# Binary cross entropy on one core: the 32-row side block is loaded at launch instead of near the end

## The chip, the core and the metric

The kernel runs on one core of a Trainium2 chip. A core has a vector engine (VectorE, DVE in the profile), a scalar engine (ScalarE, ACT), GpSimd (POOL) and a sync engine (SP); 16 DMA engines move data between HBM and the on-chip memory, SBUF, which has 128 partitions. A transfer is issued by an instruction on one engine's queue. Here those are POOL's queue (called software_dynamic in the profile, queue q0) and SP's (hardware_dynamic, q1). The metric is the time of one execution on the device in microseconds (us); lower is better.

## The reference

```
pred = np.clip(pred, eps, 1 - eps)          # eps = 1e-7
return -(target * np.log(pred) + (1 - target) * np.log(1 - pred))
```

`pred` and `target` are 8192 x 8192 float32, and so is the result. The targets are 0 or 1, so exactly one of the two logarithms counts for an element. The kernel uses this: with p the clipped prediction and t the target, |t - 1 + p| is p where t is 1, and 1 - p where t is 0. The result is minus the logarithm of that.

## The kernel before

The 67.1 million elements are cut into 37 blocks that lie one behind the other in the flat arrays. Each block is spread over 128 partitions. Blocks 0 and 1 are 7680 columns wide, blocks 2 to 33 have 15360 columns, blocks 34 and 35 again 7680, block 36 has 1696. A block of 15360 columns is 7.86 MB of float32. A remainder of 32 x 1408 elements at the very end of the arrays is the side block: it lies in two small tiles of 32 partitions, `side_p` and `side_t`.

`ring_p` (float32) and `ring_t` (bfloat16) hold two halves of 15360 columns and a small piece for block 36. Even blocks use one half and odd blocks the other. A block is worked on in place and stored from `ring_p`, so the next block that uses the same half is loaded once the store has landed.

- `load(k)` (lines 78 to 81) issues the targets on POOL's queue, which turns them into bfloat16 on the way, and the predictions, also on POOL's queue, except for block 0, whose predictions go through SP's.
- `front` (lines 98 to 106) clips on DVE (L99), adds t - 1 on DVE (L102), and takes the absolute value (L105) and the logarithm (L106) on ACT.
- `back` (L109) changes the sign on DVE.
- `store(k)` (lines 83 to 85) goes through POOL's queue, and through SP's for the last three blocks.
- `load_side` (lines 87 to 92) first writes two columns of `side_p` and `side_t` on DVE, and then issues eight loads on SP. Each moves eight rows of 1408 float32, 44 KB: rows j, j+4, ..., j+28 of the 32, for j from 0 to 3, the targets and the predictions in turn. `store_side` (lines 94 to 96) issues four such stores on SP.

The order on each engine is the order of the program text (a manual schedule). At launch the blocks 0, 1 and 2 are loaded. Blocks 0 and 1 are computed and stored, and block 3 is loaded into their half. Then the loop over blocks 2 to 32 does the front and the back of a block in two pieces, stores it, and loads block k + 2 into the same half. On POOL the store of block k, the targets of block k + 2 and the predictions of block k + 2 thus follow each other; the last one waits until the store has landed. Block 31 is the place (n - 6, with n = 37) where `load_side` is called, behind the store of that block in the text; the side block's front comes behind block 32's back, its sign change and its stores behind the first half of block 33's front. The two columns that DVE writes there keep the eight loads on SP from being issued before DVE has come to that place.

Of the kernel before, what the change touches and what calls it, by code (L numbers as in the profile page):

```python
# [1 line left out]

# [4 lines left out]

EPS = 1e-7

BIG = 15 * 1024
HALF = BIG // 2
SIDE = 1408


def plan(total):

    n, last = divmod(total, BIG)
    assert n > 4 and 0 < last <= 2048
    spots = [(HALF, 0), (HALF, HALF)]
    spots += [(BIG, k % 2 * BIG) for k in range(1, n - 1)]
    end = (n - 1) % 2 * BIG
    return spots + [(HALF, end), (HALF, end + HALF), (last - SIDE // 4, 2 * BIG)]

@with_exitstack  # L30
def kernel(
    ctx: ExitStack,
    tc: tile.TileContext,
    pred: bass.AP,
    target: bass.AP,
    out: bass.AP,
):

    nc = tc.nc
    fp32 = mybir.dt.float32
    bf16 = mybir.dt.bfloat16
    Alu = mybir.AluOpType
    Act = mybir.ActivationFunctionType
    P = nc.NUM_PARTITIONS

    R, C = pred.shape
    spots = plan(R * C // P)
    n = len(spots)
    widths = [w for w, _ in spots]
    cols = [sum(widths[:k]) for k in range(n)]

    def chunk(ap, k):
        flat = ap.rearrange("r c -> (r c)")
        return flat[cols[k] * P : (cols[k] + widths[k]) * P].rearrange("(p w) -> p w", p=P)

    pool = ctx.enter_context(tc.tile_pool(name="rings", bufs=1))
    ring = [P, 2 * BIG + widths[-1]]
    ring_p = pool.tile(ring, fp32, name="ring_p", tag="ring_p")
    ring_t = pool.tile(ring, bf16, name="ring_t", tag="ring_t")
    warm = pool.tile([1, 8], fp32, name="warm", tag="warm")
    side_p = pool.tile([32, SIDE], fp32, name="side_p", tag="side_p")
    side_t = pool.tile([32, SIDE], fp32, name="side_t", tag="side_t")

    def side(ap, j):
        flat = ap.rearrange("r c -> (r c)")  # L70
        return flat[R * C - 32 * SIDE :].rearrange("(p w) -> p w", p=32)[j:32:4]

    def spot(ring, k, part=(0, 1)):
        w, c = spots[k]
        i, m = part
        return ring[:, c + i * w // m : c + (i + 1) * w // m]

    def load(k):
        queue = nc.sync if k == 0 else nc.gpsimd
        nc.gpsimd.dma_start(out=spot(ring_t, k), in_=chunk(target, k))  # L80
        queue.dma_start(out=spot(ring_p, k), in_=chunk(pred, k))  # L81

    def store(k):
        queue = nc.sync if k >= n - 3 else nc.gpsimd
        queue.dma_start(out=chunk(out, k), in_=spot(ring_p, k))  # L85

    def load_side():
        nc.vector.memset(side_p[:, 0:2], 0.5)  # L88
        nc.vector.memset(side_t[:, 0:2], 0.0)  # L89
        for j in range(4):  # L90
            nc.sync.dma_start(out=side_t[j:32:4, :], in_=side(target, j))
            nc.sync.dma_start(out=side_p[j:32:4, :], in_=side(pred, j))

    def store_side():
        for j in range(4):
            nc.sync.dma_start(out=side(out, j), in_=side_p[j:32:4, :])

    def front_of(p, t):
        nc.vector.tensor_scalar(  # L99
            out=p, in0=p, scalar1=EPS, scalar2=1 - EPS, op0=Alu.max, op1=Alu.min  # L100
        )
        nc.vector.scalar_tensor_tensor(  # L102
            out=p, in0=t, scalar=1.0, in1=p, op0=Alu.subtract, op1=Alu.add
        )
        nc.scalar.activation(out=p, in_=p, func=Act.Abs)  # L105
        nc.scalar.activation(out=p, in_=p, func=Act.Ln)  # L106

    def back_of(p):
        nc.vector.tensor_scalar(out=p, in0=p, scalar1=-1.0, scalar2=None, op0=Alu.mult)  # L109

    def front(k, *part):
        front_of(spot(ring_p, k, *part), spot(ring_t, k, *part))

    def back(k, *part):
        back_of(spot(ring_p, k, *part))

    with tc.manual_schedule():
        nc.vector.memset(warm, 1.0)  # L118
        for k in range(3):
            load(k)  # L120
        nc.scalar.activation(out=warm, in_=warm, func=Act.Ln)  # L121
        front(0)
        front(1)
        back(0)
        store(0)
        back(1)
        store(1)
        load(3)
        for k in range(2, n - 4):
            front(k, (0, 2))  # L130
            front(k, (1, 2))
            back(k, (0, 2))
            back(k, (1, 2))
            store(k)
            if k == n - 6:
                load_side()
            if k == n - 5:
                front_of(side_p, side_t)
            for j in range(k + 2, n if k == n - 5 else k + 3):
                load(j)  # L140
        z, a, b, c = range(n - 4, n)
        front(z, (0, 2))
        back_of(side_p)
        store_side()
        front(z, (1, 2))
        back(z, (0, 2))
        front(a)
        back(z, (1, 2))
        store(z)
        front(b, (0, 2))  # L150
        front(b, (1, 2))
        back(a)
        store(a)
        front(c)
        back(b)
        store(b)
        back(c)
        store(c)


# [1 line left out]
_INS = ['pred', 'target']  # L162
_OUTS = [((8192, 8192), 'float32')]


# [23 lines left out]
```

## Time and profile before

| | us |
|---|---|
| median of 3 runs | 1864.86 |
| lowest and highest | 1864.77, 1866.35 |
| span of the profiled execution, first to last instruction | 1864.5 |
| DVE busy | 1124.7 |
| ACT busy | 902.1 |
| POOL busy | 57.6 |

The profile is of one execution, whose span is 0.4 us below the median of the runs; no other time of that execution is given. Its times count from the start of the span. A line of the timeline or of the chain of waits gives the start, the duration, the engine, the line of the kernel (L102 is line 102) and the operation with what it writes and reads; in brackets stands how long the engine had been idle and what ended that. The row "DMA" on the page cuts the span into 40 slices and gives the busy share of the 16 DMA engines in tenths (9 is 90% or more). A table of stretches gives, for each, the busy time of the engines, then the granted clock of the matrix engine (not used here), the DMA share and the GB/s moved, counted on the SBUF side, where a converted target has half its bytes. These shares are approximate, here and there a little above 1.

Of the transfers, the page shows that POOL's queue moves 657.98 MB (98.5% of the time of the 16 engines) and SP's 13.21 MB (1.7%). A load of a large prediction block takes 35.9 us from issue to landing in the median, a store 29.2 us, a load of targets 46.8 us.

### The profile page before, as it was taken

The page shows a single profiled execution, that of the slowest core. Times are in us where ns is not written, and L with a number is a line of the kernel's source. Part 1 is how long each engine was busy: PE and PEld are TensorE (multiplying, and loading weights), DVE is VectorE, ACT ScalarE, POOL GpSimd, SP SyncE. Part 2 cuts the span into 40 slices and gives each one's busy share as a digit, 9 for nine tenths or more (in the row PEclk, how much of TensorE's full clock was granted, in tenths as well). Part 3 has the DMA queues.
Part 4 walks back from the last instruction along what each step waited for, and adds up shares of the span by engine and source line. Part 5 has one row for each costly group of instructions (what it writes and reads, how often), then busy time and mean ns, then how long its engine had stood idle before and what let it go on. Part 6 is the DMA issues. An engine that isn't in the chain of part 4 may idle for free.

```text
span 1864.5 us, 649 instructions
## 1 busy us (share of the span) xinstructions
DVE 1124.7 (60%) x215; ACT 902.1 (48%) x144; POOL 57.6 (3%) x111
## 2 busy tenths in 40 slices
DVE  4655766555576655567665556766555576655585
ACT  3345553335555334555433355553335555333665
POOL 0000000000000000000000000000000000000000
DMA  9999999999999999999999999999999999999999
GB/s 295 369 355 349 348 348 368 382 385 347 351 348 348 370 380 382 343 357 344 352 370 384 386 340 356 352 345 370 382 385 345 349 355 344 371 382 386 346 341 391
DMA packets 16180, 671.22 MB, mean 360 GB/s; under 512 B 1872, under 2 KB 1872, under 8 KB 2352
## 3 DMA queue, kind: packets, MB, share of 16 engines
q0 software_dynamic: 15408, 657.98, 98.5%
q1 hardware_dynamic: 768, 13.21, 1.7%
q14 instruction: 4, 0.03, 0.0%
HBM read 536.87 MB, written 268.44 MB: 432 GB/s over the span
## 4 chain that ended last, share of the span: by engine, by line
DMA 35%; issue 26%; ACT 22%; DVE 15%; POOL 1%; DVEq 0%; POOLq 0%; PEldq 0%
DMA ring_p<-in_pred_dram 32%; ACT ring_p L105 11%; ACT ring_p L106 11%; DVE ring_p L102 7%; DVE ring_p L99 4%; DVE ring_p L109 4%; DMA out_dram<-ring_p 3%; POOL ring_t L80 0%; POOL out_dram L85 0%; DVEq L184 0%; POOL ring_p L81 0%; POOLq L85 0%; POOLq L80 0%; DVEq L99 0%; PEldq L184 0%
## 5 line engine op out<-in xcount | busy, mean ns | idle before, releaser
L105 ACT ACTIVATE ring_p<-ring_p 128x7680 f32<-128x7680 f32 (+1 forms) x70 | 450.3, 6433 | 933.6 <-DVE ring_p L102 933.6
L102 DVE SCALAR_TENSOR_TENSOR ring_p<-ring_t,ring_p 128x7680 f32<-128x7680 bf16 (+1 forms) x70 | 556.8, 7955 | 2.4
L99 DVE TENSOR_SCALAR ring_p<-ring_p 128x7680 f32<-128x7680 f32 (+1 forms) x70 | 283.8, 4054 | 398.2 <-DMA ring_p<-in_pred_dram 398.2
L109 DVE TENSOR_SCALAR ring_p<-ring_p 128x7680 f32<-128x7680 f32 (+1 forms) x69 | 283.8, 4114 | 321.2 <-ACT ring_p L106 321.2
L106 ACT ACTIVATE ring_p<-ring_p 128x7680 f32<-128x7680 f32 (+1 forms) x70 | 450.8, 6440 | 2.2
L81 POOL DMA_DIRECT2D ring_p<-in_pred_dram x36 | 19.3, 535 | 910.0 <-DMA out_dram<-ring_p 910.0
L85 POOL DMA_DIRECT2D out_dram<-ring_p x34 | 18.3, 539 | 851.7 <-DVE ring_p L109 827.4
L80 POOL DMA_DIRECT2D ring_t<-in_target_dram x37 | 20.4, 550 | 0.8 <-PEq L184 0.8
L105 ACT ACTIVATE side_p<-side_p 32x1408 f32<-32x1408 f32 x1 | 1.4, 1375 | 6.7 <-DVE side_p L102 6.7
L121 ACT ACT_TABLE_LOAD x1 | 1.3, 1283 | 0.7 <-PEq L173 0.7
L102 DVE SCALAR_TENSOR_TENSOR side_p<-side_t,side_p 32x1408 f32<-32x1408 f32 x1 | 1.6, 1611 | 0.0
L106 ACT ACTIVATE side_p<-side_p 32x1408 f32<-32x1408 f32 x1 | 1.4, 1375 | 0.0
L109 DVE TENSOR_SCALAR side_p<-side_p 32x1408 f32<-32x1408 f32 x1 | 0.9, 875 | 0.0
L99 DVE TENSOR_SCALAR side_p<-side_p 32x1408 f32<-32x1408 f32 x1 | 0.9, 874 | 0.0
L118 DVE MEMSET warm<- 1x8 f32 x1 | 0.1, 65 | 0.8 <-PEq L173 0.8
L121 ACT ACTIVATE warm<-warm 1x8 f32<-1x8 f32 x1 | 0.2, 208 | 0.0
L173 POOL MEMSET const-float32-0.0<- 128x1 f32 x1 | 0.1, 98 | 0.2 <-issue 0.2
L173 POOL MEMSET const-bfloat16-1.0<- 128x1 bf16 x1 | 0.1, 101 | 0.0
L173 POOL MEMSET const-float32-1.0<- 128x1 f32 x1 | 0.1, 98 | 0.0
L173 POOL MEMSET const-uint8-127<- 128x1 uint8 x1 | 0.1, 98 | 0.0
L88 DVE MEMSET side_p<- 32x2 f32 x1 | 0.1, 60 | 0.0
L89 DVE MEMSET side_t<- 32x2 f32 x1 | 0.1, 60 | 0.0
## 6 DMA issues: line engine op xcount, KB each, us to landing
ring_p<-in_pred_dram POOLq DMA_DIRECT2D x32, 7680.0 KB, 35.9
out_dram<-ring_p POOLq DMA_DIRECT2D x32, 7680.0 KB, 29.2
ring_t<-in_target_dram POOLq DMA_DIRECT2D x32, 3840.0 KB, 46.8
ring_p<-in_pred_dram POOLq DMA_DIRECT2D x3, 3840.0 KB, 35.7
ring_t<-in_target_dram POOLq DMA_DIRECT2D x4, 1920.0 KB, 28.1
out_dram<-ring_p POOLq DMA_DIRECT2D x2, 3840.0 KB, 27.6
out_dram<-ring_p SPq DMA_DIRECT2D x2, 3840.0 KB
ring_p<-in_pred_dram SPq DMA_DIRECT2D x1, 3840.0 KB
```

Of the source, the lines that this page charges most:

```text
L80: nc.gpsimd.dma_start(out=spot(ring_t, k), in_=chunk(target, k))
L81: queue.dma_start(out=spot(ring_p, k), in_=chunk(pred, k))
L85: queue.dma_start(out=chunk(out, k), in_=spot(ring_p, k))
L88: nc.vector.memset(side_p[:, 0:2], 0.5)
L89: nc.vector.memset(side_t[:, 0:2], 0.0)
L99: nc.vector.tensor_scalar(out=p, in0=p, scalar1=EPS, scalar2=1 - EPS, op0=Alu.max, op1=Alu.min)
L102: nc.vector.scalar_tensor_tensor(out=p, in0=t, scalar=1.0, in1=p, op0=Alu.subtract, op1=Alu.add)
L105: nc.scalar.activation(out=p, in_=p, func=Act.Abs)
L106: nc.scalar.activation(out=p, in_=p, func=Act.Ln)
L109: nc.vector.tensor_scalar(out=p, in0=p, scalar1=-1.0, scalar2=None, op0=Alu.mult)
L121: nc.scalar.activation(out=warm, in_=warm, func=Act.Ln)
L173: nc = _bacc.Bacc("TRN2", target_bir_lowering=False, num_devices=1)
```

## The change

`load_side` is called at launch, directly behind the load of block 0 and ahead of the loads of blocks 1 and 2, and no longer in the loop at block 31. The two writes of DVE in it are gone. All else stays: the same eight loads on SP's queue, the same place of the side block's computation and of its stores. Blank lines are removed, so line numbers in the changed kernel are lower: L99, L102, L105, L106 and L109 become L86, L89, L92, L93 and L96; the loads of a block become L69 and L70, its store L74, the loads of the side block L78 and L79, its stores L83.

```
     def load_side():
-        nc.vector.memset(side_p[:, 0:2], 0.5)
-        nc.vector.memset(side_t[:, 0:2], 0.0)
         for j in range(4):
             nc.sync.dma_start(out=side_t[j:32:4, :], in_=side(target, j))
             nc.sync.dma_start(out=side_p[j:32:4, :], in_=side(pred, j))
...
         nc.vector.memset(warm, 1.0)
-        for k in range(3):
-            load(k)
+        load(0)
+        load_side()
+        load(1)
+        load(2)
         nc.scalar.activation(out=warm, in_=warm, func=Act.Ln)
...
             store(k)
-            if k == n - 6:
-                load_side()
             if k == n - 5:
                 front_of(side_p, side_t)
```

## The prediction

> **What bounds the kernel now.** I read the page's busy shares first, then the slices of the span, then the chain that ended last, then the transfers by window.
>
> ```profile
> DVE 1124.7 (60%) x215; ACT 902.1 (48%) x144; POOL 57.6 (3%) x111
> ...
> DMA  9999999999999999999999999999999999999999
> ...
> HBM read 536.87 MB, written 268.44 MB: 432 GB/s over the span
> ```
>
> No compute engine is busy for more than 60% of the span, while the 16 DMA engines are at nine tenths or more in all 40 slices. The chain of waits looks at first like a loop of latencies instead. Here is one turn of it, in order of time (start, duration, what):
>
> ```profile
> 1675.80 35.94 DMA ring_p<-in_pred_dram
> 1711.76 4.17 DVE ring_p L99
> ...
> 1750.54 4.17 DVE ring_p L109
> ...
> 1755.00 29.20 DMA out_dram<-ring_p
> ...
> 1784.48 18.53 DMA ring_p<-in_pred_dram
> ```
>
> A prediction block lands, DVE and ACT work on it for 43 us, it is stored, and the store's landing frees its half of the ring for the next load. Two such loops are interleaved, one for each half. Whether the loop or the bandwidth sets the pace is told by the stretches of one block each (length, DVE, ACT, POOL busy, clock, DMA share, GB/s):
>
> ```profile
> 57.00:78.00 21.00, 4.61 (x2) 8.74 (x2) 1.48 (x3) 1.00 1.01 413
> ...
> 97.00:151.00 54.00, 31.98 (x7) 25.45 (x4) 1.16 (x3) 1.00 0.98 357
> ...
> 1567.00:1621.00 54.00, 32.53 (x7) 25.97 (x5) 1.61 (x3) 1.00 1.01 364
> ...
> 1676.00:1730.00 54.00, 32.51 (x9) 25.94 (x5) 1.39 (x3) 1.00 1.00 364
> ```
>
> The DMA share is 0.98 to 1.01 at the start, in the middle and in the stretch that now holds the side loads. So the 28 and 36 us in the loop are time in a queue that never runs dry. One block reads 7.86 MB of predictions and 7.86 MB of targets (float32 in HBM, halved on the way in) and writes 7.86 MB; 23.59 MB in the steady period of 54.35 us is 434 GB/s. All 805.3 MB at that rate take 1855.5 us. The rest of the 1864.5 us span is accounted for: about 1.5 us before the first packet (three empty slices of 0.5 us when the transfers are cut to the first 20), 3.7 us of missing DMA share in the last 18.5 us (80.1% there), and a wobble of 3.4 us early on. That wobble is in the issues of the prediction loads on POOL:
>
> ```profile
> 96.31 0.54 POOL L81 DMA_DIRECT2D ring_p<-in_pred_dram  x1 [24.98 <-DMA out_dram<-ring_p]
> ...
> 150.92 0.54 POOL L81 DMA_DIRECT2D ring_p<-in_pred_dram  x1 [29.05 <-DMA out_dram<-ring_p]
> ...
> 206.19 0.53 POOL L81 DMA_DIRECT2D ring_p<-in_pred_dram  x1 [29.44 <-DMA out_dram<-ring_p]
> ...
> 697.59 0.53 POOL L81 DMA_DIRECT2D ring_p<-in_pred_dram  x1 [29.08 <-DMA out_dram<-ring_p]
> ...
> 1675.80 0.53 POOL L81 DMA_DIRECT2D ring_p<-in_pred_dram  x1 [28.41 <-DMA out_dram<-ring_p]
> ...
> 1730.16 0.53 POOL L81 DMA_DIRECT2D ring_p<-in_pred_dram  x1 [28.46 <-DMA out_dram<-ring_p]
> ```
>
> The periods are 54.6, then 55.3 us; from 96.31 to 697.59 eleven of them take 601.3 us against 597.9 at 54.35, which is 3.4 us more. Afterwards they are steady. In the trace's landing marks (16 for each block transfer, one for each DMA engine) the engines are within 1.1 us of each other in the first transfers and within 3.9 us from 600 us on: the wobble lasts while they drift apart.
>
> **The change, part by part.**
>
> *Bytes.* None are added or removed. Moving 360 KB inside a queue that is never empty costs 0, unless it makes the queue run empty somewhere, or changes the wobble or the uneven finish.
>
> *What the near end loses.* Eight DMA issues on SP (0.62 to 0.79 us each, 5.5 us, from 1700.39) and eight transfers. Their cost on the DMA engines is in the window 1695 to 1745 us (packets, MB, share of 16 engines):
>
> ```profile
> q1 hardware_dynamic: 128, 0.36, 1.8%
> ```
>
> This is 64 data packets, eight to a load, and 64 completion marks: 1.8% of 16 x 50 us is 14.4 us, 1.8 us on each of eight engines. On the path it costs nothing now: the store issued at 1700.63 lands 29.5 us later, as its neighbours do, and the distance from the load issue at 1675.80 to the one at 1730.16 is 54.36 us, against 54.35 without side loads. The other eight engines were the later ones by more than 1.8 us (the spread was 3.9), so the eight that carry the side loads had room. Credit at the end: 0, at most 1.8.
>
> *What the launch gets.* The eight issues now stand on SP behind the load of pred block 0 (issued at 0.74). Seven go at once, about 4.6 us of SP time. The eighth reuses block 0's semaphore and waits until block 0 has landed (19.65 us). Behind that wait on SP there is only the store of the side block, now issued at 1779.28, so nobody feels it. POOL's queue keeps its order: targets 0 and 1, pred 1, target 2 and pred 2 go out between 1.24 and 4.0 us as before. The side packets lie behind pred 0 in the same queue, so the landing of pred 0 does not move. After it they take turns with POOL's packets on eight engines: 7 x 0.22 = 1.6 us, and 0.2 for the eighth.
>
> Target 0 landed at about 22.0 us by its marks, and its first reader (L102) starts at 23.84, behind L99 on DVE: 1.8 us of room for at most 1.6. Pred 1 (40.15 us) can come up to 1.8 us late if the side's engines finish it last; since the 16 marks lie within 1.1 us then, they would. Then front(1), back(0) and store(0) (56.86) and store(1) (70.26) are up to 1.8 us late too. The cover is the queue: target 2 and pred 2 keep the engines busy until 77.55, the 57 to 78 row has a share of 1.01, so store 0 is 20.7 us early for the queue. If that cover were gone, the 1.8 us would be idle time and stay in the result. In the steady state the thinnest point is at a store's issue (1755.00), when the last prediction load lands at 1766.10: 11 us of queued bytes against a lag of 1.8.
>
> *The memsets.* Two of 60 ns leave DVE at 1700.28. The wait of store 31 that ends on one of them gets 0.1 us shorter, in front of a queue that is full: 0.
>
> *The sum.* End 0 (between -1.8 and 0), launch 0 (between 0 and +1.8), memsets 0, wobble 0 (between -3.4, when it vanishes, and +3.4, when it doubles). I take 0 for launch and end together, by the nearest row: the very same eight loads moved the landing times by 0.01 us, and an engine that gets its 1.8 us early doesn't get them late. Profiled span 1864.5 us; the median of the runs, 1864.86, is 0.4 above it and holds what lies around the span. Forecast 1864.9 us.
>
> One rule speaks against the change. The Trainium skill, DMA: Bandwidth & Descriptors, section Rules for kernel authors, says that transfers under 64 KB pay mostly overhead; its section Anatomy of one DMA gives about 2.0 us fixed for each (fitted for GpSimd's path). By that, as an estimate, eight 44 KB loads in front of pred 1 cost 16 us and the time is 1881. The 54.36 us period with all eight in it is against this: here the fixed part is latency that other packets fill.
>
> **The rivals.**
>
> *A, the lag passes through.* The loop of latencies would be the real bound, and pred 1 and pred 2, 1.8 us late, shift everything while the near end gives nothing back: 1866.7 us. For it: the unbroken chain through loads, compute and stores. Against it: DMA shares of 1.0 in every block's stretch.
>
> *B, the wobble goes.* The eight side engines start 1.8 us apart from the others, which is half the final 3.9 us of drift, so the slow early periods need not happen. The four long ones (55.27, 55.01, 54.91 and 55.02) hold 2.8 of the 3.4 us: 1862.1 us, 1861.5 with all of it. Against it: each half of the engines still starts in step.
>
> *C, slower: the wobble never settles.* If two groups 1.8 us apart keep meeting where loads give way to stores, the early average (3.4 / 11 = 0.31 us a period) stays for the other 20 periods (31 in all up to the issue at 1784.48): +6.2 us, 1871.1. It decides, by over 0.2%, from 3.7 / 20 = 0.19 us a period. Against it: drift stopped by itself at 3.9 us, and a delayed engine only drifts further.
>
> That the change doesn't do what it says is hardly open: no wait stands in front of the seven loads, and the eighth's ends at 20 us.
>
> **How the numbers follow.** Forecast 0.70 (1864.9), A 0.12 (1866.7), B 0.07 (1862.1), C 0.11 (1871.1). What a measurement of this kernel can tell from no change is about 0.2%, 3.7 us: below 1861.1 or above 1868.6. Forecast, A and most of B lie within it. Faster 0.04 (B with an evener finish, part of those 3.7 us), slower 0.12 (C, and A with a larger wobble), same 0.84. The range goes from B's 1862.1 up to A's 1866.7 plus the 1.6 us by which the three runs differ: 1868.3. C is left out.
>
> **What would show it.** Side loads on SP from about 1.1 us, the eighth near 20; pred 1 landing between 40.2 and 42.0; the first stores late by as much; load issues 54.3 to 54.4 us apart at 1600 us and on; DMA share near 1.0 in every stretch. The prediction is wrong if a stretch falls clearly under 0.98 after the launch (the queue ran dry), or if the steady period is above 54.5 us (C).

## The result, and the profile after

The changed kernel takes 1868.2 us (median of 21 runs, 1867.08 to 1872.34), the kernel before 1865.59 us (21 runs, 1864.67 to 1867.29). The ratio is 1.0017, with a 95% interval from 1.0011 to 1.0023: the change costs about 2.6 us. The forecast was 1864.9, no change. The time lies inside the stated range and the difference is under the 0.2% that I had called the limit of a measurement, but these runs do tell the kernels apart. Of the four cases of the prediction, the two that make the kernel slower are rivals A (0.12) and C (0.11).

The page of the changed kernel, with the rows for the engines, the DMA slices and HBM:

```profile
DVE 1124.7 (60%) x213; ACT 902.1 (48%) x144; POOL 57.4 (3%) x111
...
DMA  9999999999999999999999999999999999999998
...
HBM read 536.87 MB, written 268.44 MB: 431 GB/s over the span
```

DVE and ACT work exactly as long as before and the DMA engines are as full; only the span is longer, 1868.4 us. Each run's list now gives its time and its span, and the time is 1.7 to 1.9 us above the span in every one. So the profiled execution took 1870.19 us, 2 us more than the median, and the profiled one of the kernel before (span 1864.5) must have been the 1866.35 us one, not one near the median: the "0.4 us around the span" of my sum was wrong. The two profiles thus show 3.9 us, more than the difference of the medians, 2.6.

SP's timeline, as start, duration and operation, shows the moved loads:

```profile
1.19 0.79 SPq L78 DMA_DIRECT2D side_t<-in_target_dram  x1
...
5.38 0.62 SPq L78 DMA_DIRECT2D side_t<-in_target_dram  x1
19.51 0.62 SPq L79 DMA_DIRECT2D side_p<-in_pred_dram  x1
1782.91 2.75 SPq L83 DMA_DIRECT2D out_dram<-side_p  x4
```

The first stands at 1.19 us, the seventh at 5.38, and the eighth has waited until block 0 landed, at 19.51. The next lines are POOL's issues of prediction loads. The bracket says how long POOL waited and for what, here for the store of the block two before; a store has landed when its last DMA engine is done.

```profile
97.45 0.54 POOL L70 DMA_DIRECT2D ring_p<-in_pred_dram  x1 [24.96 <-DMA out_dram<-ring_p]
...
151.51 0.53 POOL L70 DMA_DIRECT2D ring_p<-in_pred_dram  x1 [28.48 <-DMA out_dram<-ring_p]
...
205.92 0.53 POOL L70 DMA_DIRECT2D ring_p<-in_pred_dram  x1 [28.46 <-DMA out_dram<-ring_p]
...
480.11 0.53 POOL L70 DMA_DIRECT2D ring_p<-in_pred_dram  x1 [29.41 <-DMA out_dram<-ring_p]
...
535.29 0.53 POOL L70 DMA_DIRECT2D ring_p<-in_pred_dram  x1 [29.97 <-DMA out_dram<-ring_p]
...
590.40 0.53 POOL L70 DMA_DIRECT2D ring_p<-in_pred_dram  x1 [29.20 <-DMA out_dram<-ring_p]
...
1407.02 0.53 POOL L70 DMA_DIRECT2D ring_p<-in_pred_dram  x1 [28.41 <-DMA out_dram<-ring_p]
...
1462.18 0.53 POOL L70 DMA_DIRECT2D ring_p<-in_pred_dram  x1 [29.23 <-DMA out_dram<-ring_p]
...
1679.43 0.53 POOL L70 DMA_DIRECT2D ring_p<-in_pred_dram  x1 [28.40 <-DMA out_dram<-ring_p]
...
1733.77 0.53 POOL L70 DMA_DIRECT2D ring_p<-in_pred_dram  x1 [28.41 <-DMA out_dram<-ring_p]
```

Three differences between such lines make up the whole span. The issue for block 3 stands at 97.45 us, 1.14 later than before (96.31). From there to the issue for block 33 there are 30 periods: 1636.32 us, against 1633.85 before (1730.16 - 96.31) and 1630.5 at 54.35 us each. So the excess of the 30 periods is 5.8 us instead of 3.35, 2.47 more. Of that, 0.7 us is one event, of which the last section tells: the period from 1407.02 to 1462.18 is 55.16 us, the next one 54.21. The rest lies in periods up to 590 us (55.33, 55.18 and 55.11 us among them), where the kernel before was nearly steady, and in single ones of up to 54.84 us until 1081 us. What follows block 33's issue takes 134.63 us instead of 134.34. 1.14 + 2.47 + 0.29 = 3.9 us.

The rate of the steady periods is unchanged: 54.34 us between the last two lines. One turn of the loop in the chain of waits is as before too, a load of 35.95 us and a store of 29.39:

```profile
1679.43 35.95 DMA ring_p<-in_pred_dram
...
1715.40 4.17 DVE ring_p L86
...
1758.64 29.39 DMA out_dram<-ring_p
...
1788.32 18.57 DMA ring_p<-in_pred_dram
```

So are the DMA shares by stretch (length, DVE, ACT and POOL busy, clock, DMA share, GB/s):

```profile
57.00:78.00 21.00, 4.88 (x2) 9.89 (x2) 1.61 (x3) 1.00 0.98 399
97.00:151.00 54.00, 32.43 (x7) 25.86 (x5) 1.60 (x3) 1.00 1.00 362
1567.00:1621.00 54.00, 32.51 (x7) 25.95 (x5) 1.60 (x3) 1.00 1.01 364
1676.00:1730.00 54.00, 32.52 (x7) 25.95 (x5) 1.60 (x3) 1.00 1.00 362
1811.00:1829.00 18.00, 16.27 (x5) 9.60 (x2) 0.54 (x1) 1.00 0.96 372
```

In the last row the share falls to 0.96. The same stretch of the kernel before, 4 us earlier in its own time:

```profile
1807.00:1825.00 18.00, 16.25 (x5) 9.47 (x2) 0.54 (x1) 1.00 1.03 386
```

Some DMA engines stood idle there, waiting for the store that POOL issues at 1823.70 us. By the landing marks it was the engines that were ahead (their lead over the last one shrinks from 7.0 to 4.9 us in that store), so this cost the result nothing; but it shows that the engines had moved apart. The marks, 16 to a transfer, show how. In the last transfer before the side block's stores, counted back from the last mark, they stand at 0 and 2.7 to 3.3 us (eight engines) and at 6.1 to 6.4 us (the other eight). In the kernel before they are spread from 0 to 3.7 us without groups. When the side block's stores run, the first eight fall back by 0.7 us against the other eight. So the engines of the first group are the ones that carry the side block, and the last of all is one of them.

The Trainium skill, DMA: Bandwidth & Descriptors, section Why a DMA increments its semaphore by 16 and not by 1, says that a transfer uses the largest number of engines, up to 16, that divides its slowest dimension on both sides (here the rows), and that one issued on SP takes the lowest-numbered of them. The records agree as far as they go: eight packets to a load of eight rows, and after eight such loads two groups of eight marks. They carry no engine numbers, so that these are the lowest-numbered ones isn't shown.

### The profile page after: what moved, and what is told of

Read it like the earlier page. It is cut to its first block, busy times and chain, and to the rows that moved or that the text cites. A ratio compares the mean times of both kernels' runs of the same rounds, so it can differ in the third digit from the quotient of the medians.

```text
span 1868.4 us, 647 instructions
## 1 busy us (share of the span) xinstructions
DVE 1124.7 (60%) x213; ACT 902.1 (48%) x144; POOL 57.4 (3%) x111
## 4 chain that ended last, share of the span: by engine, by line
DMA 35%; issue 26%; ACT 22%; DVE 15%; POOL 1%; DVEq 0%; POOLq 0%; PEldq 0%
DMA ring_p<-in_pred_dram 32%; ACT ring_p L92 11%; ACT ring_p L93 11%; DVE ring_p L89 7%; DVE ring_p L86 4%; DVE ring_p L96 4%; DMA out_dram<-ring_p 3%; POOL ring_t L69 0%; POOL out_dram L74 0%; DVEq L171 0%; POOL ring_p L70 0%; POOLq L74 0%; POOLq L69 0%; DVEq L86 0%; PEldq L171 0%
## 5 line engine op out<-in xcount | busy, mean ns | idle before, releaser
L92 ACT ACTIVATE ring_p<-ring_p 128x7680 f32<-128x7680 f32 (+1 forms) x70 | 450.3, 6433 | 937.5 <-DVE ring_p L89 937.5
L89 DVE SCALAR_TENSOR_TENSOR ring_p<-ring_t,ring_p 128x7680 f32<-128x7680 bf16 (+1 forms) x70 | 556.9, 7955 | 2.4
L86 DVE TENSOR_SCALAR ring_p<-ring_p 128x7680 f32<-128x7680 f32 (+1 forms) x70 | 283.8, 4055 | 402.0 <-DMA ring_p<-in_pred_dram 402.0
L96 DVE TENSOR_SCALAR ring_p<-ring_p 128x7680 f32<-128x7680 f32 (+1 forms) x69 | 283.8, 4115 | 321.2 <-ACT ring_p L93 321.2
L93 ACT ACTIVATE ring_p<-ring_p 128x7680 f32<-128x7680 f32 (+1 forms) x70 | 450.8, 6440 | 2.2
L70 POOL DMA_DIRECT2D ring_p<-in_pred_dram x36 | 19.2, 532 | 913.8 <-DMA out_dram<-ring_p 913.8
L74 POOL DMA_DIRECT2D out_dram<-ring_p x34 | 18.4, 541 | 852.0 <-DVE ring_p L96 852.0
L69 POOL DMA_DIRECT2D ring_t<-in_target_dram x37 | 20.0, 542 | 0.8 <-PEq L171 0.8
L92 ACT ACTIVATE side_p<-side_p 32x1408 f32<-32x1408 f32 x1 | 1.4, 1375 | 6.7 <-DVE side_p L89 6.7
L89 DVE SCALAR_TENSOR_TENSOR side_p<-side_t,side_p 32x1408 f32<-32x1408 f32 x1 | 1.6, 1614 | 0.0
L93 ACT ACTIVATE side_p<-side_p 32x1408 f32<-32x1408 f32 x1 | 1.4, 1375 | 0.0
L86 DVE TENSOR_SCALAR side_p<-side_p 32x1408 f32<-32x1408 f32 x1 | 0.9, 875 | 0.0
L96 DVE TENSOR_SCALAR side_p<-side_p 32x1408 f32<-32x1408 f32 x1 | 0.9, 874 | 0.0
L105 DVE MEMSET warm<- 1x8 f32 x1 | 0.1, 65 | 0.8 <-PEq L160 0.8
```

Of the source, the lines that this page charges most:

```text
L86: nc.vector.tensor_scalar(out=p, in0=p, scalar1=EPS, scalar2=1 - EPS, op0=Alu.max, op1=Alu.min)
L89: nc.vector.scalar_tensor_tensor(out=p, in0=t, scalar=1.0, in1=p, op0=Alu.subtract, op1=Alu.add)
```

## The experiments

Each kernel was timed beside the kernel before, on one chip, and profiled once; the landing marks and packet records come from these profiles. "Slow packets" are the 61,440-byte packets of the large blocks that took over 2.33 us; the usual one takes 2.267. Their extra time, divided by 16, is 2.9 us per engine in the kernel before and 4.2 us in the changed one. By their times they start about 5 us before a prediction load lands, which would be its second-to-last packet on an engine, on many engines at once, and most of them stand before 700 us.

Theory 1 at the start: the time is that of the last DMA engine. Near the end, the eight carriers of the side block have room, since the engines have drifted 3.9 us apart; at launch they have none, and fall behind for good.

**The side block left out.**

```
-            if k == n - 6:
-                load_side()
-            if k == n - 5:
-                front_of(side_p, side_t)
...
-        back_of(side_p)
-        store_side()
```

> The side block is left out (its rows of the result are not computed), all else as before the change. Theory 1 (the time is that of the last of the 16 DMA engines; the side loads and stores of the kernel before fall on engines that have room): 0 to -0.5 us against the kernel before, since the side block costs it nothing. Rival 2 (each engine's work counts alike wherever it stands): -2.7 us, the side block's 12 packets of 0.22 us on each of its eight engines.

1865.07 us against 1865.85 (ratio 0.9995, 0.9986 to 1.0004): -0.8 us. By the medians, the side block's 2.7 us on each of eight engines cost the kernel before less than a third of that. Rival 2 (-2.7 us, ratio 0.9986) is at the very edge of the interval. In the profiles, 0.7 us of the difference lie behind the issue for block 33 (134.34 us before, 133.66 here), where the side block's stores run.

**Loads of 16 rows at launch.** The changed kernel with:

```
-        for j in range(4):
-            nc.sync.dma_start(out=side_t[j:32:4, :], in_=side(target, j))
+        for j in range(2):
+            nc.sync.dma_start(out=side_t[j:32:2, :], in_=side(target, j, 2))
```

and the same for the predictions, with `side` taking every second row.

> The side block is loaded at launch, but in four loads of 16 rows instead of eight of 8, so that all 16 DMA engines should carry 0.9 us of it and none 1.8. Theory 1 (eight engines put 1.8 us behind the others before the drift are the ones that end last): the landing marks show no two groups, and the time is 0.9 us or less over the kernel before (1865.6 to 1866.5), well under the changed kernel's 1868.2. Rival 3 (anything at launch that makes prediction block 1 late costs the same): like the changed kernel, +1.5 to +2.6.

1866.01 against 1865.85 us (1.0000, 0.9992 to 1.0009). With the same bytes at the same place, spread over 16 engines, the median loses 0.2 us (the interval reaches from -1.5 to +1.7), and ten of the eleven runs lie below 1867.08 us, the lowest of the changed kernel's 21. The landing marks show no two groups (0 to 3.8 us, one by one, at the same place as above). POOL's issues for blocks 3 and 33:

```profile
96.88 0.54 POOL L70 DMA_DIRECT2D ring_p<-in_pred_dram  x1 [24.78 <-DMA out_dram<-ring_p]
...
1730.16 0.53 POOL L70 DMA_DIRECT2D ring_p<-in_pred_dram  x1 [28.44 <-DMA out_dram<-ring_p]
```

Block 3 is 0.57 us late, and the 30 periods take 1633.28 us, 0.57 less than before.

**Late first blocks without any transfer.** The kernel before, with DVE work between the two DVE operations of block 1's front:

```
+        if wait:
+            nc.vector.memset(side_p, 0.5)
+            for _ in range(4):
+                back_of(side_p)
         nc.vector.scalar_tensor_tensor(
...
-        front(1)
+        front(1, wait=True)
```

> The kernel before, with about 4 us of work on DVE put into the front of block 1 (between its two DVE operations), so that the stores of blocks 0 and 1 come some 4 us late; no transfer is added. Theory 1: 0 (the queue is full until 77 us). Rival A of the prediction (a late first block passes through the chain of waits to the end): +4.

1865.95 against 1865.71 us (1.0000, 0.9992 to 1.0009). DVE's and POOL's timelines of it:

```profile
44.38 1.23 DVE L103 MEMSET side_p<- 32x1408 f32 x1 [0.23 <-issue]
45.64 3.63 DVE L113 TENSOR_SCALAR side_p<-side_p 32x1408 f32<-32x1408 f32 x4
```

```profile
61.70 0.54 POOL L85 DMA_DIRECT2D out_dram<-ring_p  x1 [57.68 <-DVE ring_p L113]
75.09 0.54 POOL L85 DMA_DIRECT2D out_dram<-ring_p  x1 [12.85 <-DVE ring_p L113]
...
96.44 0.54 POOL L81 DMA_DIRECT2D ring_p<-in_pred_dram  x1 [20.27 <-DMA out_dram<-ring_p]
...
1730.66 0.53 POOL L81 DMA_DIRECT2D ring_p<-in_pred_dram  x1 [28.43 <-DMA out_dram<-ring_p]
```

The stores of blocks 0 and 1 are 4.8 us late (56.86 and 70.26 before), and the load of block 3 goes out at 96.44, 0.13 late. A late block alone is absorbed by the queue, as the prediction said. So the 1.14 us of the changed kernel aren't a late block that passes through the chain; they are engines that are behind.

**The place of the loads.** The kernel before with `if k == n - 6:` (block 31) changed to `if k == 3:`, then to `if k == 14:`, and with k == 14 once more as loads of 16 rows.

> The kernel before, with the side loads called at block 3 (about 175 us) instead of block 31, with its two writes on DVE. Theory 1: the engines have drifted by about 1.6 us only, so eight of them fall behind as at launch: +1.5 to +2.6 us. Rival 3 (only the launch counts, through a late prediction block 1): 0.

> The kernel before, with the side loads called at block 14 (about 775 us), where the periods have become steady. Theory 1: 0 to +0.5 us against the kernel before, as at block 31. Rival 2 and rival 3: 0 as well; a rival by which the near end alone hides the loads (1.8 us spent anywhere else counts): +1.8.

> The side loads at block 14, as four loads of 16 rows, so that all 16 engines get 0.9 us each and keep their distances. Theory 1 with what the first run at block 14 adds to it (moving eight engines by 1.8 us brings engines into step that had drifted apart, and they are slow again): 0 to +0.4 us against the kernel before, below the +1.2 of the eight-row loads there, and no slow packets behind block 14. Rival (the place alone counts): +1.2 again.

Block 3: 1867.33 us, +1.5 (1.0008, 0.9999 to 1.0016). Block 14: 1867.08, +1.2 (1.0007, 0.9998 to 1.0016). Block 14 with 16 rows: 1867.15, +1.4 (1.0004, 0.9995 to 1.0013). None is clear of no change, and none is clear of 1 to 2 us either. The early place came out at the low end of what I expected. At block 14 I had expected next to nothing, and the 16-row loads were to be cheaper than the 8-row loads there; both medians missed. That expectation had left out that 16-row loads give every engine, the last one too, 0.9 us. In their profile the cost stands in one place: the period with the loads in it, from 751.70 to 807.71 us, is 56.01 us, with over 20 slow packets of up to 2.9 us at 780 to 784 us, and behind it there are none but the one at 1446 us. At launch the same loads cost 0.2 us by the medians; the interval there doesn't exclude 0.9.

**One, two and four sets of loads at launch, and half a set.** The changed kernel again; with `load_side()` called twice; four times; and with the columns cut in two, 0 to 703 at launch and 704 to 1407 at block 31:

```
         load(0)
-        load_side()
+        for _ in range(4):
+            load_side()
```

```
-        load_side()
+        load_side(0)
...
+            if k == n - 6:
+                load_side(SIDE // 2)
```

> The changed kernel once more, beside the other three on one chip. Theory 1 (the eight engines that carry the side loads are put 1.8 us behind before the drift, and one of them ends last) and its rivals: +1.5 to +3 us against the kernel before, as measured.

> The changed kernel with its eight side loads issued twice at launch, so that eight engines carry 3.6 us there and not 1.8. Theory 1: 1.8 us more than the changed kernel, +4 to +4.8 against the kernel before; two groups in the landing marks about 3.5 us apart from the start. Rival 4 (the cost is the longer stretch of slow packets, while engines of a group stay in step): no more than the changed kernel, +2 to +3, since the groups themselves are as tight as there.

The changed kernel again: 1868.65 against 1865.71 us, +2.9 (1.0016, 1.0007 to 1.0025). Two sets: 1868.74, +3.0 (1.0016, 1.0007 to 1.0025). Theory 1's +4 to +4.8 failed, and rival 4's number held, but not its reason, as POOL's lines for two sets show:

```profile
99.22 0.54 POOL L70 DMA_DIRECT2D ring_p<-in_pred_dram  x1 [25.88 <-DMA out_dram<-ring_p]
...
153.47 0.53 POOL L70 DMA_DIRECT2D ring_p<-in_pred_dram  x1 [28.66 <-DMA out_dram<-ring_p]
...
209.13 0.54 POOL L70 DMA_DIRECT2D ring_p<-in_pred_dram  x1 [29.73 <-DMA out_dram<-ring_p]
...
263.49 0.53 POOL L70 DMA_DIRECT2D ring_p<-in_pred_dram  x1 [28.44 <-DMA out_dram<-ring_p]
...
317.83 0.54 POOL L70 DMA_DIRECT2D ring_p<-in_pred_dram  x1 [28.40 <-DMA out_dram<-ring_p]
...
1731.38 0.53 POOL L70 DMA_DIRECT2D ring_p<-in_pred_dram  x1 [28.40 <-DMA out_dram<-ring_p]
```

Block 3 is 2.9 us late, twice the delay of one set and more. But the periods are steady from 209 us on (54.36, 54.34), and all 30 take 1632.16 us, 1.7 less than before. The two groups of engines stand 3 us apart from about 210 us on, and after that there are no slow packets but single ones. Each group is no looser than in the changed kernel (seven of the carriers within 0.4 us), so being in step with seven others isn't what makes packets slow. The two groups don't overlap in the changed kernel either, from launch on, and its slow packets go on until 1060 us, when the gap between the groups has grown to about 3 us too (in its second profile they all but end at 466 us, at a gap of 2.4). That gave theory 5: lag and slow packets are traded against each other until the halves are about 3 us apart; beyond that, lag counts in full. The profile is of one of the shorter runs (1867.8 us), so these lines show 1.5 us more than before, not the 3.0 of the medians.

> The eight side loads are issued four times at launch: 7.2 us on each of eight engines instead of 1.8 (double: 3.6). Theory 5 (the time is that of the last engine, a carrier of side packets: its side packets plus its own slow packets; the slow packets end once the two halves of the engines are over about 3 us apart, so lag and slow packets are traded against each other up to there, and beyond that lag counts in full): +3.6 us over the doubled loads less at most 1.5 us of slow packets still to be saved, +5 to +6.6 against the kernel before. Rival 4 (the cost is not the lag): +3 again, as with one and two sets.

> The side loads are cut in two by columns: columns 0 to 703 of all eight at launch, 704 to 1407 at block 31 behind the writes on DVE. No byte is added, the carriers fall 0.9 us behind at launch instead of 1.8. Theory 5: between the two kernels, +0.8 to +2. Rival 4 (any launch traffic on the eight engines sets off the long stretch of slow packets): +2.6 to +3, as the changed kernel.

Four sets: 1873.45 against 1865.70 us, +7.8 (1.0043, 1.0029 to 1.0058; five runs, 1871.67 to 1876.65). Rival 4 is out. Theory 5's 5 to 6.6 was low. POOL's lines of it:

```profile
101.77 0.54 POOL L70 DMA_DIRECT2D ring_p<-in_pred_dram  x1 [28.38 <-DMA out_dram<-ring_p]
...
1734.44 0.53 POOL L70 DMA_DIRECT2D ring_p<-in_pred_dram  x1 [28.41 <-DMA out_dram<-ring_p]
```

Block 3 is 5.5 us late, and the 30 periods take 1632.67 us, 1.2 less than before, but 0.5 more than with two sets. By the marks the gap between the halves of the engines is over 3 us here from 81 us on and over 5 at 101 us, and yet slow packets come until about 250 us, and single ones later; so the end of the slow packets at a gap of 3 us, on which theory 5 rests, isn't shown. This profile, too, is of one of the shorter runs (1871.86 us): it shows 5.5 us of the 7.8.

Half a set: 1867.84, +2.1 (1.0010, 1.0001 to 1.0020), just above theory 5's range and within 1 us of rival 4's; it doesn't decide between them. But its lines show two things:

```profile
96.15 0.54 POOL L70 DMA_DIRECT2D ring_p<-in_pred_dram  x1 [24.55 <-DMA out_dram<-ring_p]
...
1677.32 0.54 POOL L70 DMA_DIRECT2D ring_p<-in_pred_dram  x1 [28.40 <-DMA out_dram<-ring_p]
...
1732.44 0.53 POOL L70 DMA_DIRECT2D ring_p<-in_pred_dram  x1 [29.19 <-DMA out_dram<-ring_p]
```

Eight loads at launch, of half the bytes, don't make block 3 late at all (96.31 before), so it isn't the number of loads that delays, but the bytes (0.9 us of packets to an engine, no more than the 0.6 to 1.1 us by which the engines differ there anyway). And the half that is loaded near the end, from 1701.94 us on, costs 0.8 us (the period is 55.12 us), while all eight loads cost the kernel before 0.01 us at the same place.

In one table, from each profile: the issue for block 3, the excess of 30 periods over 1630.5 us, what follows block 33's issue, and beside them the difference of the medians, which are over 5 to 33 runs (a span is that of one execution, and can lie up to 2 us off the median):

```
kernel                 block 3   excess    rest     span   median against before
before                  96.31     3.35   134.34   1864.5
16 rows at launch       96.88     2.78   133.94   1864.1    +0.2
DVE 4.9 us late         96.44     3.72   133.64   1864.3    +0.2
side left out           96.51     2.53   133.66   1863.2    -0.8
at block 3              96.29     4.02   134.59   1865.4    +1.5
at block 14             96.14     3.83   134.53   1865.0    +1.2
at block 14, 16 rows    96.33     4.62   133.95   1865.4    +1.4
half at launch          96.15     5.79   134.76   1867.2    +2.1
changed kernel          97.45     5.82   134.63   1868.4    +2.6
changed, again          97.23     3.86   134.61   1866.2    +2.9
two sets                99.22     1.66   134.62   1866.0    +3.0
four sets              101.77     2.17   135.56   1870.0    +7.8
```

The first column follows the lag of the carriers from a full set on. The second is a matter of luck with the slow packets: the changed kernel's two profiles differ by 2 us in it, and its runs scatter more widely too (5.3 us from lowest to highest, against 2.6 before). The third holds the side block's four stores, 0.9 us on each of the same eight engines: it is 133.64 us where they cost next to nothing (with the DVE delay; 133.66 without the side block) and 134.5 to 135.6 wherever 8-row loads run ahead of block 31. On the average of the changed kernel's two profiles, against the one of before, the launch costs 1.0 us, the periods 1.5 us (0.7 of it the event at 1446 us, in both) and the rest 0.3: 2.8 us, as the medians have it.

## Why the prediction was wrong

- *What bounds the kernel*: right. The steady period is 54.34 us again, and in the stretches shown up to block 32 the share is 0.98 or more; the 0.96 behind them is that of engines which are ahead. DMA bandwidth is the bound, and a late first block is absorbed.
- *What moves*: right in the details. Pred 1 is used at 41.30 us (40.15 before; "between 40.2 and 42.0"), stores 0 and 1 are 1.2 us late, and the memsets' going shows nowhere.
- *The cover*: right for the first block, wrong as an answer. A full queue hides lateness of a block. It doesn't hide work that is added to some of the 16 engines, since each has its own share of every transfer, and a transfer lands with the last.
- *The step that failed*: "I take 0 for launch and end together ... an engine that gets its 1.8 us early doesn't get them late." That is true of the engine and false of the time. The time is that of the last engine, and the carriers aren't the last engines in both cases. Near the end they had up to 3.9 us of room, and leaving the side block out altogether gains only 0.8 us. Even there the reading "the other eight engines were the later ones" was too simple: after the loads three marks still lie 3.1 to 3.7 us ahead of the last, which no engine that had just lost 1.8 of 3.9 us could, while the last three lie within 0.24 us; the loads had used up nearly all the room, and the side stores behind them moved the last mark by 0.7 us. At launch the spread is 0.7 to 1.1 us; the 1.8 us stick out by 1.14 (0.92 in the second profile), and the periods that follow give nothing back in either. I had both spreads in the text, and used the later one only to explain why the near end is free.
- *The wobble*: left at 0 between -3.4 and +3.4; it measured +2.5 in one profile and +0.5 in the other, 0.7 of each by the event at 1446 us. Rival C was right that it lasts longer in the first (to about 590 us, and in single periods to 1081) and wrong that it might never settle. Rival B, that it goes, happens by half with two sets, where the lag eats the gain.
- *Rival A* came nearest in size, +1.8 against 2.6, for a wrong reason: no latency passes through the chain, as the DVE delay shows.
- *The estimate against the change* (16 us, 2.0 for each of eight small loads): the runs show 2.6 us, and 0.2 us for the same bytes in four loads over 16 engines, so no fixed cost of that size was paid for each load.
- *The profiled execution*: 1.8 us, not 0.4, lie around the span. Since I forecast the median itself, this moved nothing, but the profile of before was one of the longer ones.

Not settled: what makes packets near the end of a prediction load slow, and with it why the changed kernel's periods lose 0.5 us against the kernel before in one execution and 2.5 in another; and the cost at block 14. No version here beats the kernel before: the best that computes everything, 16 rows at launch, is level with it.

## What to carry to other kernels

When the DMA engines are the bound, as here, the time is that of the last of the 16, not their average. A transfer that uses only some of them is free only while those engines are ahead: look at how far apart the landing marks of one transfer lie at the place where the transfer would go, and which engines it uses. Work that must be early goes over all 16 engines; work for a few belongs where these have gained room.

## What the runs showed that I had not expected

- The engines don't stay in step by themselves. From 0.6 to 1.1 us at launch they drift to 3 to 6 us apart, by packets that take 2.4 to 3.9 us instead of 2.267, nearly always near the end of a prediction load; once they are apart, some 20 periods in a row agree within 0.1 us.
- In 11 of the 12 profiles shown or told of here one single packet of about 2.64 us stands at the same time, some 1446 us into the span. It hits one engine. In the changed kernel this was the last one: the period from 1407.02 to 1462.18 is 55.16 us. In the kernel before it was an engine with room, and POOL's lines show nothing:

```profile
1404.09 0.53 POOL L81 DMA_DIRECT2D ring_p<-in_pred_dram  x1 [28.42 <-DMA out_dram<-ring_p]
...
1458.42 0.53 POOL L81 DMA_DIRECT2D ring_p<-in_pred_dram  x1 [28.42 <-DMA out_dram<-ring_p]
```

  This is 54.33 us. The same event costs up to 0.8 us or nothing, by which engine it meets. That goes with the place of the loads: in all six profiles with 8-row loads at launch or at block 3 that period is 54.84 to 55.17 us, in the other six, one of which lacks the packet, 54.33 to 54.35. Putting eight engines last thus made this packet count, for 0.4 to 0.7 us; which engine it hits, the records don't say.
- An engine that leads by too much gets nothing from it: with a lead of 5 to 7 us it runs out of queued work near the end, in the changed kernel's 0.96 above.
